# Hi and lo of the latent up-projections staged in the attention's probability tiles as well, until the first latent head begins

## The chip, the core and the metric

The kernel runs on one core of one Trainium2 chip. The metric is the device time of one execution in microseconds. A profile is one execution recorded by the hardware profiler. Engines are named as in the profile: PE is TensorE's matmuls, PEld its weight loads, DVE VectorE, ACT ScalarE, POOL GpSimd, and SP the engine whose queue issues nearly all transfers.

## What is computed

A two-layer encoder over two sequences of 512 tokens (width 1024). The first layer mixes with grouped-query and differential attention, the second with latent attention; each layer then has cross attention to a memory and a gated feed-forward part. The change lies in the latent attention of the second layer:

```python
def mla(h, w_in, g_q, g_kv, w_uq, w_ukv, ang):
    a = h @ w_in
    cq, ckv, kr = jnp.split(a, [C_Q_RANK, C_Q_RANK + C_KV_RANK], axis=-1)
    q = (rms_norm(cq, g_q) @ w_uq).reshape(B, S, C_HEADS, C_NOPE + C_ROPE)
    qn, qr = q[..., :C_NOPE], rope(q[..., C_NOPE:], ang)
    kv = (rms_norm(ckv, g_kv) @ w_ukv).reshape(B, S, C_HEADS, C_NOPE + C_VDIM)
    kn, v = kv[..., :C_NOPE], kv[..., C_NOPE:]
    ...
    # per head: softmax((qn kn + qr kr) * scale) @ v, 16 heads
```

## The kernel before

Activations lie transposed, features on the partitions and 512 tokens along the free dimension; `b` is the sequence. Every float32 operand x is kept as two parts, hi (x rounded) and lo (x minus hi), and a product is three matmuls: hi hi, hi lo, lo hi (`gemm`, `gemm_k`, L126 to L128 and L738 to L740). A product ends in one of three PSUM tiles (`pg`).

The latent stage runs so. `mla_in` projects down and normalises. `mla_up` then makes, for each quarter `u` of the heads, the queries (`qn`, four products of 9 matmuls of 512 columns), for every second quarter the rotated query parts (`rope_q`, four products of 9), the keys (`keys`, four products of 6) and the values (`values`, four products of 12 matmuls of 256 columns, each evicted in two halves). The rotated parts pass through f tiles: two multiplications on DVE and a sum on POOL each. Every result is split into hi and lo in one staging tile (tag `hl`): ACT writes hi, DVE writes lo (L817 and L818, L96 and L97, L848 and L849), and SP then stores the tile to DRAM, from where the heads load it again in another layout. The `hl` tag has two buffers of 128 x 1024 floats. A quarter takes 20 of these tiles: 4, 4, 4 and 8.

The first quarter runs alone (`until(up, lambda: 0 in done)`); the other quarters are woven into the heads of sequence 0. A head (`attend64`) takes four query blocks: scores into one of two `pss` tiles (L909 to L911), the minimum on DVE (L433), the exponential on ACT (L436), scaling on POOL (L441), transposes on PE (L447), hi and lo of the transposed probabilities into two tiles of tag `pt` (L449, L450), and the product with the values (L479, L481). Tag `pt` has four buffers of the same 128 x 1024 floats. Before the heads, `mla_in` uses them for three projections and, at its two ends, for the spread of the norms (`e`).

The order of instructions on each engine is fixed when the kernel is built: the Tile framework schedules the program against a timeline that it models, so a change in buffers moves instructions of several engines. Each engine and the SP queue then work strictly in that order. A wait for a tile that still has to be stored is the wait for its last transfer to land.

Of the kernel before, what the change touches and what calls it, by code (L numbers as in the profile page):

```python
# [10 lines left out]
F32R = mybir.dt.float32r  # L11
# [8 lines left out]
T = 512  # L20
# [14 lines left out]
def trunk_kernel(ctx, tc, xt, memt, gains, lams, w_in0, w_out0, w_in1, w_uq, w_ukv, w_out1,  # L35
# [21 lines left out]
    def nm(s):  # L57
        uid[0] += 1
        return f"{s}{uid[0]}"
# [5 lines left out]
    def f_tile():  # L65
        return f_p.tile([128, T], F32, tag="f", name=nm("f"))
# [9 lines left out]
    def raw(ap):  # L76
        return ap.bitcast(F32)
# [17 lines left out]
    def split(hi, lo, f, eng=None):  # L95
        nc.scalar.copy(hi, f)  # L96
        (eng or nc.vector).tensor_tensor(out=lo, in0=f, in1=raw(hi), op=SUB)  # L97
# [4 lines left out]
    def load_w(src, n=1024, first=False, key=None):  # L102
        r = wr_p.tile([128, 1024], F32, tag="wr", name=nm("wr"))
        h = wh_p.tile([128, 1024], F32R, tag="wh", name=nm("wh"))
        l = wl_p.tile([128, 1024], F32R, tag="wl", name=nm("wl"))
        if key in los:
            dma(r, src)
            dma(raw(l), los.pop(key))
            nc.scalar.copy(h, r)
            return lambda i, n=1: (h[:, i * 128:(i + n) * 128], l[:, i * 128:(i + n) * 128])  # L110
        step = 256 if first else n
        for c in range(0, n, step):
            cs = slice(c, c + step)
            dma(r[:, cs], src[:, cs])
            nc.scalar.copy(h[:, cs], r[:, cs])  # L115
            (nc.vector if first else nc.gpsimd).tensor_tensor(out=l[:, cs], in0=r[:, cs],  # L116
                                                              in1=raw(h[:, cs]), op=SUB)
        if key is not None:
            los[key] = d = dram([128, 1024])
            dma(d, raw(l))  # L120
        return lambda i, n=1: (h[:, i * 128:(i + n) * 128], l[:, i * 128:(i + n) * 128])

    def gemm(ps, ws, xs):
        n = len(ws)
        for i, ((wh, wl), (xh, xl)) in enumerate(zip(ws, xs)):
            nc.tensor.matmul(ps, lhsT=wh, rhs=xh, start=(i == 0), stop=False)  # L126
            nc.tensor.matmul(ps, lhsT=wh, rhs=xl, start=False, stop=False)  # L127
            nc.tensor.matmul(ps, lhsT=wl, rhs=xh, start=False, stop=(i == n - 1))  # L128
# [221 lines left out]
    def cross_kv(l, at):  # L350
# [6 lines left out]
        for m in range(KC):  # L357
            w = load_w(w_ckv[l, m])
            p = pg()
            gemm(p, [w(k) for k in range(KC)], mem)  # L360
            f = f_tile()
            nc.vector.tensor_tensor(out=f, in0=p, in1=Rm[0], op=MUL)
            hl, hi, lo = hl2(at)
            split(hi, lo, f)
            kd[l][m] = d = dram([128, 2, T])
            dma(d, raw(hl))
            yield 5.2
# [141 lines left out]
    skB = [[dram([128, 2, T]) for _ in range(4)] for _ in range(2)]  # L509
    svB = [[dram([2, 128, T]) for _ in range(4)] for _ in range(2)]  # L510

    def hl2(at):
        x = at.tile([128, 2 * T], F32R, tag="hl", name=nm("hl"), bufs=2)
        return x, x[:, :T], x[:, T:]

    def tt(eng, out, a, b, op):
        eng.tensor_tensor(out=out, in0=a, in1=b, op=op)  # L517
# [219 lines left out]
    def gemm_k(o, wh, wl, xh, xl, first, last, **k):  # L737
        nc.tensor.matmul(o, lhsT=wh, rhs=xh, start=first, stop=False, **k)  # L738
        nc.tensor.matmul(o, lhsT=wh, rhs=xl, start=False, stop=False, **k)  # L739
        nc.tensor.matmul(o, lhsT=wl, rhs=xh, start=False, stop=last, **k)  # L740
# [68 lines left out]
        return c_hl  # L809

    def mla_up(at, c_hl, done):
        def qn(w, i, j):
            for b in range(2):
                p = pg()
                gemm(p, [w(i * 3 + k) for k in range(3)], c_hl[b][0:3])
                hl, hi, lo = hl2(at)
                nc.scalar.activation(hi, p, AF.Copy, scale=MLA_SCALE)  # L817
                nc.vector.scalar_tensor_tensor(out=lo, in0=p, scalar=MLA_SCALE, in1=raw(hi),  # L818
                                               op0=MUL, op1=SUB)
                dma(sqn[b][j], raw(hl))  # L820
                yield 1.95

        def keys(w, i, j):
            for b in range(2):
                p = pg()
                gemm(p, [w(i * 2 + k) for k in range(2)], c_hl[b][3:5])
                hl, hi, lo = hl2(at)
                split(hi, lo, p)
                dma(skn[b][j], raw(hl))
                yield 1.4  # L830

        def values(w, u):

            wv = [w(4 + 2 * k, 2) for k in range(2)]
            for b in range(2):
                for tp in range(2):
                    p = pg()
                    for j in range(2):
                        t = tp * 2 + j
                        for k in range(2):  # L840
                            xh, xl = (x[:, t * 128:(t + 1) * 128] for x in c_hl[b][3 + k])
                            gemm_k(p[:, j * 256:(j + 1) * 256], xh, xl, *wv[k], k == 0, k == 1)
                    for j in range(2):
                        t = tp * 2 + j
                        x = at.tile([128, 2 * T], F32R, tag="hl", name=nm("hl"), bufs=2)[:, :T]
                        xv = x.rearrange("p (h s e) -> p h s e", h=4, s=2)
                        pv = p[:, j * 256:(j + 1) * 256].rearrange("p (h e) -> p h e", h=4)
                        nc.scalar.copy(xv[:, :, 0], pv)  # L848
                        nc.vector.tensor_tensor(out=xv[:, :, 1], in0=pv, in1=raw(xv[:, :, 0]),  # L849
                                                op=SUB)  # L850
                        dma(svn[b][u][:, :, t * 128:(t + 1) * 128].rearrange("h p c -> p h c"),
                            raw(x).rearrange("p (h c) -> p h c", h=4))
                    yield 1.4

        def rope_q(g):
            w = load_w(w_uq[4 + g][:, :768], 768)
            cs = at.tile([128, 2 * T], F32, tag="kk", name=nm("ropeC"), bufs=2)
            cos, sin = cs[:, :T], cs[:, T:]
            dma(cos, rope_c[0])
            dma(sin, rope_c[1])  # L860
            for b in range(2):
                eo = []
                for i in range(2):
                    p = pg()
                    gemm(p, [w(i * 3 + k) for k in range(3)], c_hl[b][0:3])
                    eo.append(p)
                for i in range(2):
                    x, y = f_tile(), f_tile()
                    tt(nc.vector, x, eo[i], cos, MUL)
                    tt(nc.vector, y, eo[1 - i], sin, MUL)  # L870
                    tt(nc.gpsimd, x, x, y, SUB if i == 0 else ADD)
                    hl, hi, lo = hl2(at)
                    split(hi, lo, x)
                    dma(sqr[b][g][:, i], raw(hl))
                yield 3.9

        for u in range(4):
            j = 2 * u
            w = load_w(w_uq[j // 2][:, :768], 768)
            for i in range(2):  # L880
                yield from qn(w, i, j + i)
            if u % 2 == 0:
                yield from rope_q(u // 2)
            w = load_w(w_ukv[j // 2])
            for i in range(2):
                yield from keys(w, i, j + i)
            yield from values(w, u)
            done.append(u)
# [425 lines left out]
    with ExitStack() as es:  # L1314
        at = es.enter_context(tc.tile_pool(name="at0", bufs=4))
# [12 lines left out]
        done = []  # L1328
# [14 lines left out]
    with ExitStack() as es:  # L1343
        at = es.enter_context(tc.tile_pool(name="at1", bufs=4))
        nq[0], nv[0] = 4, 2
        c_hl = mla_in(at)
        done = []
        up = mla_up(at, c_hl, done)
        o = [[], []]
        until(up, lambda: 0 in done)  # L1350
        kr = mla_kr(at, 0)
        for u in range(4):
            until(up, lambda: u in done)
            weave(mla_attn(at, 0, kr, range(2 * u, 2 * u + 2), o[0], "B"), up, 1.0)
        first = proj_residual(0, w_out1, ("mix", 1), o[0], next_x(0, G_CROSS + 8, "C"))
        weave(mla_attn(at, 1, mla_kr(at, 1), range(8), o[1], "A"), first, 0.30)
        ops = XOps(1)
        oc = after_mixing(at, 1, w_out1, o, first, ops)
# [123 lines left out]
```

## Time and profile before

| | |
|---|---|
| time, median of 3 runs | 3066.44 us (3065.6 to 3070.57) |
| profiled execution, its own time | 3070.69 us |
| profiled execution, span of its instructions | 3068.9 us |
| PE busy | 2936.0 us, 96% of the span |
| DVE, ACT, POOL busy | 66%, 45%, 54% |
| granted TensorE clock, mean | 0.983 |
| DMA | 500 MB, 163 GB/s over the span |

The profiled execution's own time is what compares with the runs; its span leaves out about 2 us around the first and last instruction. Positions below are microseconds from the span's start. The latent up-projections begin at about 1694 us, the first latent scores at 1739 us, and the last heads end at about 2140 us.

### The profile page before, as it was taken

To read this page: it belongs to the slowest core of one execution; us is meant where nothing else is said; L and a number is where in the kernel's file an instruction comes from. 1 tells how busy PE (TensorE), PEld (TensorE's weight loads), DVE (VectorE), ACT (ScalarE), POOL (GpSimd) and SP (SyncE) were. 2 spreads that over 40 slices of the span, in tenths; PEclk is the share of its full clock that TensorE was granted. 3 is DMA by queue.
4 is the path that set the end of the run, shared out by engine and by line. 5 is a ranking of instruction groups with operands and counts; after the bars stand their busy time and mean duration, and the time that the engine had idled before them with its cause. 6 is when DMAs were issued, how large, how long until landed. Compare 5 with 4: busy or idle time off the path is not lost. (4 is left out here: it accounts for less than half of the span.)

```text
span 3068.9 us, 42037 instructions
## 1 busy us (share of the span) xinstructions
PE 2936.0 (96%) x14301; PEld 2425.2 (79%) x14301; DVE 2029.7 (66%) x3417; ACT 1391.6 (45%) x2610; POOL 1654.2 (54%) x1222
## 2 busy tenths in 40 slices
PE   8999999999999999998999799999999999999996
PEld 6878899877887888876777688888887788887775
DVE  7566766665467665678774576666458666669776
ACT  3245456545344333343343366656444333334342
POOL 5453445443256666667674343553355666666665
PEclk9999999999999999999999999999999999999998
DMA  3554554656573222245341677764756222226442
GB/s 137 166 174 158 189 206 141 228 194 207 185 244 110 103 103 103 103 153 174 132 161 65 209 270 262 241 209 158 247 189 216 96 103 103 99 98 208 138 152 81
DMA packets 217958, 500.01 MB, mean 163 GB/s; under 512 B 22800, under 2 KB 48784, under 8 KB 217744
## 3 DMA queue, kind: packets, MB, share of 16 engines
q1 hardware_dynamic: 217600, 497.28, 47.2%
q8 instruction: 114, 1.87, 0.2%
q14 instruction: 100, 0.82, 0.1%
q10 hardware_dynamic: 144, 0.04, 0.0%
HBM read 341.00 MB, written 156.24 MB: 162 GB/s over the span
## 5 line engine op out<-in xcount | busy, mean ns | idle before, releaser
L126 PE MATMUL pg<-u,wh 128*128 128x512 f32 x1360 | 541.6, 400 | 19.8 <-DVE hl L97 5.2
L128 PE MATMUL pg<-u,wl 128*128 128x512 f32 x1360 | 538.7, 397 | 7.1 <-DMA wl<-dram 4.7
L127 PE MATMUL pg<-u,wh 128*128 128x512 f32 x1360 | 539.1, 397 | 5.2 <-DVE u L242 4.8
L441 POOL TENSOR_SCALAR p<-p,rs 128x512 f32<-128x512 f32 (+1 forms) x288 | 190.6, 665 | 461.0 <-DVE rs L437 380.3
L116 POOL TENSOR_TENSOR wl<-wr,wh 128x1024 fp32r<-128x1024 f32 (+1 forms) x112 | 275.8, 2464 | 271.0 <-ACT wh L115 264.0
L96 ACT CAST s<-ws 128x512 fp32r<-128x512 f32 (+2 forms) x304 | 170.5, 563 | 331.6 <-POOL ws L517 112.2
L126 PEld LDWEIGHTS pg<-u,wh 128*128 128x128 f32 x1360 | 258.6, 190 | 78.7 <-DVE hl L818 6.6
L128 PEld LDWEIGHTS pg<-u,wl 128*128 128x128 f32 x1360 | 257.8, 190 | 61.4 <-DMA wl<-dram 6.2
L127 PEld LDWEIGHTS pg<-u,wh 128*128 128x128 f32 x1360 | 257.9, 190 | 60.0 <-DVE u L242 9.5
L97 DVE TENSOR_TENSOR s<-ws,s 128x512 fp32r<-128x512 f32 x176 | 175.8, 1000 | 90.9 <-ACT s L96 90.9
L436 ACT ACTIVATE p<-p,mx 128x512 f32<-128x512 f32 (+1 forms) x256 | 171.5, 670 | 111.1 <-DVE mx L433 103.6
L449 ACT CAST ptt<-pt 128x512 fp32r<-128x512 f32 (+1 forms) x288 | 151.4, 536 | 130.4 <-PE pt L447 128.7
L450 DVE TENSOR_TENSOR ptt<-pt,ptt 128x512 fp32r<-128x512 f32 (+1 forms) x288 | 177.6, 624 | 39.7 <-ACT ptt L449 38.0
L738 PE MATMUL pss<-u,s 128*128 128x512 f32 x484 | 191.7, 397 | 6.9 <-ACT s L96 3.4
L237 POOL TENSOR_TENSOR ssq<-ssq,f 128x512 f32<-128x512 f32 x100 | 149.3, 1497 | 90.6 <-ACT f L235 88.0
L740 PE MATMUL pss<-u,s 128*128 128x512 f32 x484 | 192.3, 397 | 1.1 <-DVE s L97 1.1
L517 POOL TENSOR_TENSOR f<-f,c 128x512 f32<-128x512 f32 x88 | 148.6, 1690 | 81.4 <-DVE f L517 78.3
L739 PE MATMUL pss<-u,s 128*128 128x512 f32 x484 | 191.7, 396 | 0.0
L115 ACT CAST wh<-wr 128x1024 fp32r<-128x1024 f32 (+2 forms) x120 | 118.5, 993 | 160.9 <-PE pg L127 105.3
L97 POOL TENSOR_TENSOR s<-ws,s 128x384 fp32r<-128x384 f32 (+1 forms) x128 | 145.2, 1141 | 76.7 <-ACT s L96 75.4
L738 PE MATMUL pg<-u,s 128*128 128x512 f32 x440 | 175.3, 398 | 6.2 <-ACT s L96 2.8
L739 PE MATMUL pg<-u,s 128*128 128x512 f32 x440 | 174.5, 397 | 2.0 <-DVE u L517 2.0
(300 smaller groups left out, 7840.5 us busy)
## 6 DMA issues: line engine op xcount, KB each, us to landing
dram<-hl SPq DMA_DIRECT2D x88, 512.0 KB, 3.0
wr<-in_w_gu_dram SPq DMA_DIRECT2D x88, 512.0 KB, 3.3
u<-dram SPq DMA_DIRECT2D x154, 256.0 KB, 3.6
dram<-f SPq DMA_DIRECT2D x152, 256.0 KB, 2.7
kk<-dram SPq DMA_DIRECT2D x52, 512.0 KB, 4.9
q<-dram SPq DMA_DIRECT2D x96, 256.0 KB, 4.3
dram<-wl SPq DMA_DIRECT2D x48, 512.0 KB, 2.9
wl<-dram SPq DMA_DIRECT2D x48, 512.0 KB, 4.3
```

Source lines behind the costliest of these rows:

```text
L96: nc.scalar.copy(hi, f)
L97: (eng or nc.vector).tensor_tensor(out=lo, in0=f, in1=raw(hi), op=SUB)
L116: (nc.vector if first else nc.gpsimd).tensor_tensor(out=l[:, cs], in0=r[:, cs], in1=raw(h[:, cs]), op=SUB)
L126: nc.tensor.matmul(ps, lhsT=wh, rhs=xh, start=(i == 0), stop=False)
L127: nc.tensor.matmul(ps, lhsT=wh, rhs=xl, start=False, stop=False)
L128: nc.tensor.matmul(ps, lhsT=wl, rhs=xh, start=False, stop=(i == n - 1))
L436: nc.scalar.activation(p, p, AF.Exp, bias=mn, scale=-1.0, accum_out=su)
L441: nc.gpsimd.tensor_scalar(out=p, in0=p, scalar1=rs, scalar2=1.0, op0=MUL, op1=MUL)
L450: nc.vector.tensor_tensor(out=pl, in0=tv, in1=raw(ph), op=SUB)
L738: nc.tensor.matmul(o, lhsT=wh, rhs=xh, start=first, stop=False, **k)
L739: nc.tensor.matmul(o, lhsT=wh, rhs=xl, start=False, stop=False, **k)
L740: nc.tensor.matmul(o, lhsT=wl, rhs=xh, start=False, stop=last, **k)
```

## The change

`mla_up` takes its staging tiles through a counter. While no quarter is done (`done` is empty, which is the first quarter's 20 tiles), two of three tiles are taken from the four buffers of tag `pt` and the third from the two of `hl`; later quarters use `hl` alone, as before. The arithmetic stays as it is.

```diff
--- before.py
+++ after.py
@@ -509,8 +509,8 @@
     skB = [[dram([128, 2, T]) for _ in range(4)] for _ in range(2)]
     svB = [[dram([2, 128, T]) for _ in range(4)] for _ in range(2)]
 
-    def hl2(at):
-        x = at.tile([128, 2 * T], F32R, tag="hl", name=nm("hl"), bufs=2)
+    def hl2(at, tag="hl"):
+        x = at.tile([128, 2 * T], F32R, tag=tag, name=nm("hl"), bufs=4 if tag == "pt" else 2)
         return x, x[:, :T], x[:, T:]
 
     def tt(eng, out, a, b, op):
@@ -809,11 +809,18 @@
         return c_hl
 
     def mla_up(at, c_hl, done):
+
+        turn = [0]
+
+        def up_hl():
+            turn[0] += 1
+            return hl2(at, "pt" if not done and turn[0] % 3 else "hl")
+
         def qn(w, i, j):
             for b in range(2):
                 p = pg()
                 gemm(p, [w(i * 3 + k) for k in range(3)], c_hl[b][0:3])
-                hl, hi, lo = hl2(at)
+                hl, hi, lo = up_hl()
                 nc.scalar.activation(hi, p, AF.Copy, scale=MLA_SCALE)
                 nc.vector.scalar_tensor_tensor(out=lo, in0=p, scalar=MLA_SCALE, in1=raw(hi),
                                                op0=MUL, op1=SUB)
@@ -824,7 +831,7 @@
             for b in range(2):
                 p = pg()
                 gemm(p, [w(i * 2 + k) for k in range(2)], c_hl[b][3:5])
-                hl, hi, lo = hl2(at)
+                hl, hi, lo = up_hl()
                 split(hi, lo, p)
                 dma(skn[b][j], raw(hl))
                 yield 1.4
@@ -842,7 +849,7 @@
                             gemm_k(p[:, j * 256:(j + 1) * 256], xh, xl, *wv[k], k == 0, k == 1)
                     for j in range(2):
                         t = tp * 2 + j
-                        x = at.tile([128, 2 * T], F32R, tag="hl", name=nm("hl"), bufs=2)[:, :T]
+                        x = up_hl()[0][:, :T]
                         xv = x.rearrange("p (h s e) -> p h s e", h=4, s=2)
                         pv = p[:, j * 256:(j + 1) * 256].rearrange("p (h e) -> p h e", h=4)
                         nc.scalar.copy(xv[:, :, 0], pv)
@@ -869,7 +876,7 @@
                     tt(nc.vector, x, eo[i], cos, MUL)
                     tt(nc.vector, y, eo[1 - i], sin, MUL)
                     tt(nc.gpsimd, x, x, y, SUB if i == 0 else ADD)
-                    hl, hi, lo = hl2(at)
+                    hl, hi, lo = up_hl()
                     split(hi, lo, x)
                     dma(sqr[b][g][:, i], raw(hl))
                 yield 3.9
```

The built order of the instructions moves with it. Names are tile and number; `hl_16373`, `hl_16387`, `hl_16401`, `hl_16415` are the staging tiles of the first four query products (`pg_16363` to `pg_16405`), and `hl_16249`, `hl_16289` those of the key rotation at the end of `mla_in`. Lines of the changed kernel are 7 higher from here on.

ACT at the start of the up-projections, before:

```order
L96 CAST hl_16289<-f_16285 32x512
L817 ACTIVATE hl_16373<-pg_16363 128x512
L196 COPY r_16328<-pa_16323 128x512
L196 COPY r_16335<-pt_16330 128x512
L96 CAST u_16338<-c_16086 128x512
L817 ACTIVATE hl_16387<-pg_16377 128x512
L96 CAST u_16343<-c_16150 128x512
L115 CAST wh_16505<-wr_16504 128x1024
L96 CAST u_16348<-c_16140 128x512
L817 ACTIVATE hl_16401<-pg_16391 128x512
L96 CAST u_16353<-c_16205 128x512
```

and in the changed kernel:

```order
L824 ACTIVATE hl_16373<-pg_16363 128x512
L824 ACTIVATE hl_16387<-pg_16377 128x512
L96 CAST hl_16289<-f_16285 32x512
L824 ACTIVATE hl_16401<-pg_16391 128x512
L196 COPY r_16328<-pa_16323 128x512
L196 COPY r_16335<-pt_16330 128x512
L96 CAST u_16338<-c_16086 128x512
L115 CAST wh_16505<-wr_16504 128x1024
L96 CAST u_16343<-c_16150 128x512
L824 ACTIVATE hl_16415<-pg_16405 128x512
```

The first three query evictions now stand together, ahead of the copies of the norms (L196) and the splits of the key and value latents (`u`); before, the second to fourth stood between those.

PE where the first latent scores (`pss_16672`, head 0, block 0) begin; `pg_16596` is the third product of the first quarter's values, `pg_16691` the second query product of the second quarter. Before:

```order
L739 MATMUL pg_16596<-wl_16506,u_16353 128x256
L740 MATMUL pg_16596<-wh_16505,u_16354 128x256
L909 MATMUL pss_16672<-kk_16662,q_16661 128x512
L910 MATMUL pss_16672<-kk_16662,q_16661 128x512
L911 MATMUL pss_16672<-kr_16658,q_16663 128x512
```

and in the changed kernel:

```order
L127 MATMUL pg_16691<-u_16077,wh_16639 128x512
L128 MATMUL pg_16691<-u_16076,wl_16640 128x512
L916 MATMUL pss_16672<-kk_16662,q_16661 128x512
L917 MATMUL pss_16672<-kk_16662,q_16661 128x512
L918 MATMUL pss_16672<-kr_16658,q_16663 128x512
```

Three products moved ahead of the first scores: the fourth of the values (`pg_16617`) and two of the second quarter's queries (`pg_16644`, `pg_16691`).

ACT where the first exponentials stand (`p_16679` is head 0, block 0; `hl_16567` to `hl_16634` are the eight halves of the first quarter's values). Before:

```order
L96 CAST hl_16550<-pg_16543 128x512
L848 CAST hl_16567<-pg_16554 128x4x64
L436 ACT_TABLE_LOAD
L436 ACTIVATE p_16679,su_16677<-p_16679,mx_16676 128x512
L436 ACTIVATE p_16712,su_16710<-p_16712,mx_16709 128x512
L848 CAST hl_16571<-pg_16554 128x4x64
```

and in the changed kernel:

```order
L855 CAST hl_16592<-pg_16575 128x4x64
L115 CAST wh_16842<-wr_16841 128x1024
L855 CAST hl_16609<-pg_16596 128x4x64
L855 CAST hl_16613<-pg_16596 128x4x64
L855 CAST hl_16630<-pg_16617 128x4x64
L436 ACT_TABLE_LOAD
L436 ACTIVATE p_16679,su_16677<-p_16679,mx_16676 128x512
L824 ACTIVATE hl_16654<-pg_16644 128x512
```

The exponentials stood behind the first of the eight value halves and now stand behind the seventh (`hl_16630`), with the split of a weight tile (`wh_16842`) between.

## Rows read from the trace of the kernel before

**Rows 1.** The page of the profiled execution: its span, and its part 1 (busy time of each engine, its share of the span, its instructions).

```profile
span 3068.9 us, 42037 instructions
...
PE 2936.0 (96%) x14301; PEld 2425.2 (79%) x14301; DVE 2029.7 (66%) x3417; ACT 1391.6 (45%) x2610; POOL 1654.2 (54%) x1222
```

**Rows 2.** Busy time by stretch, a stretch per row: its length, then for PE, PEld, DVE, ACT and POOL the busy us and, in brackets, the instructions, then the granted TensorE clock (1.00 is full), the mean busy share of the 16 DMA engines, and GB/s.

```profile
1700.00:1740.00 40.00, 27.58 (x120) 21.02 (x119) 20.73 (x30) 12.40 (x21) 12.63 (x8) 0.87 0.63 218
1740.00:1780.00 40.00, 36.17 (x200) 29.32 (x199) 25.50 (x68) 26.27 (x58) 13.80 (x16) 1.00 0.78 264
...
1850.00:1950.00 100.00, 94.55 (x564) 81.05 (x562) 66.19 (x176) 65.43 (x149) 38.95 (x46) 0.98 0.71 236
1950.00:2050.00 100.00, 100.00 (x551) 85.75 (x550) 66.94 (x156) 64.48 (x125) 61.32 (x50) 1.00 0.72 248
```

**Rows 3.** Waits of PE between 1693 and 1746 us: the matmul that waited, by tile and line, what released it, us in total, times, the longest.

```profile
PE pg L126 <- DVE hl L97: 5.2, 1, 5.2
PE pg L126 <- DVE hl L818: 4.4, 3, 2.3
PE pg L738 <- DVE hl L97: 2.3, 1, 2.3
PE pss L909 <- DVE mx L433: 1.4, 1, 1.4
PE pt L447 <- POOL p L441: 1.1, 1, 1.1
```

**Rows 4.** PE in order of time: start, us, engine, line, operation, tiles, forms, and in brackets the idle time ahead of it with its releaser. The matmuls of 128x512 follow each other in one product, so the distance of two starts is what one costs.

```profile
1702.87 0.50 PE L126 MATMUL pg<-u,wh 128*128 128x512 f32 x1 [1.40 <-DVE hl L818]
...
1707.49 0.50 PE L126 MATMUL pg<-u,wh 128*128 128x512 f32 x1 [2.28 <-DVE hl L818]
...
1708.30 0.39 PE L126 MATMUL pg<-u,wh 128*128 128x512 f32 x1
1708.53 0.40 PE L127 MATMUL pg<-u,wh 128*128 128x512 f32 x1
...
1713.02 0.50 PE L126 MATMUL pg<-u,wh 128*128 128x512 f32 x1 [0.71 <-DVE hl L818]
...
1727.56 0.80 PE L126 MATMUL pg<-u,wh 128*128 128x512 f32 x1 [5.16 <-DVE hl L97]
...
1729.01 0.63 PE L126 MATMUL pg<-u,wh 128*128 128x512 f32 x1
1729.43 0.63 PE L127 MATMUL pg<-u,wh 128*128 128x512 f32 x1
...
1732.76 0.58 PE L738 MATMUL pg<-wh,u 128*128 128x256 f32 x1 [2.27 <-DVE hl L97]
...
1738.26 0.28 PE L739 MATMUL pg<-wl,u 128*128 128x256 f32 x1
1738.38 0.28 PE L740 MATMUL pg<-wh,u 128*128 128x256 f32 x1
...
1738.86 0.39 PE L909 MATMUL pss<-kk,q 128*128 128x512 f32 x1
...
1745.67 0.66 PE L447 MATMUL pt<-ident,p 128*128 128x128 f32 x4 [1.08 <-POOL p L441]
```

**Rows 5.** ACT in order of time, same columns: two evictions into the staging tile, and the first exponential of the latent attention.

```profile
1731.39 0.58 ACT L96 CAST hl<-pg 128x512 fp32r<-128x512 f32 x1 [4.62 <-DMA dram<-hl]
...
1742.13 0.37 ACT L848 CAST hl<-pg 128x256 fp32r<-128x256 f32 x1 [6.11 <-DMA dram<-hl]
...
1743.81 0.72 ACT L436 ACTIVATE p<-p,mx 128x512 f32<-128x512 f32 x1
```

**Rows 6.** Busy time by stretches of 4 us, columns as in rows 2.

```profile
1722.00:1726.00 4.00, 0.40 (x2) 0.00 (x0) 1.02 (x2) 0.62 (x1) 1.45 (x1) 1.00 0.74 239
1726.00:1730.00 4.00, 2.44 (x6) 1.83 (x6) 0.69 (x1) 0.58 (x1) 0.00 (x0) 0.53 1.02 322
...
1738.00:1742.00 4.00, 3.90 (x21) 2.78 (x19) 1.39 (x4) 0.00 (x0) 0.00 (x0) 1.00 0.84 335
```

**Rows 7.** DMA issues between 1700 and 1746 us: destination and source, queue, count, KB each, median us from issue to landing.

```profile
dram<-hl SPq DMA_DIRECT2D x12, 512.0 KB, 3.5
kk<-dram SPq DMA_DIRECT2D x3, 512.0 KB, 4.6
q<-dram SPq DMA_DIRECT2D x5, 256.0 KB, 5.3
```

**Rows 8.** DVE and then POOL in order of time, columns as in rows 4: evictions, rotations and a weight split of the up-projections.

```profile
1712.28 0.69 DVE L818 SCALAR_TENSOR_TENSOR hl<-pg,hl 128x512 fp32r<-128x512 f32 x1 [2.36 <-ACT hl L817]
1712.88 3.23 DVE L517 TENSOR_TENSOR f<-pg,ropeC 128x512 f32<-128x512 f32 x5
1716.28 1.12 DVE L97 TENSOR_TENSOR hl<-f,hl 128x512 fp32r<-128x512 f32 x1 [0.17 <-ACT hl L96]
...
1714.31 2.54 POOL L517 TENSOR_TENSOR f<-f,f 128x512 f32<-128x512 f32 x2 [1.18 <-DVE f L517]
...
1719.49 2.29 POOL L116 TENSOR_TENSOR wl<-wr,wh 128x768 fp32r<-128x768 f32 x1
```

**Rows 9.** Waits of PE between 1746 and 2290 us, columns as in rows 3: the two largest.

```profile
PE pss L909 <- DMA kk<-dram: 3.1, 2, 2.2
PE pa L479 <- ACT ptt L449: 2.7, 4, 2.0
```

## The prediction, made before the changed kernel ran

> **What bounds the kernel now.** I read the page first: PE is busy 2936.0 of 3068.9 us [rows 1], so the kernel is bound by PE, and an edit is worth what it takes from PE's idle time or slow clock. The busy time by stretch shows where that lies [rows 2]: in the 40 us from 1700 PE is busy only 27.58 us and its clock is granted at 0.87, the worst stretch near the change; from 1950 to 2050 PE is busy without a break, so what is won ahead of 1950 has nothing to be lost in there. Third, the waits of PE around 1700 [rows 3]: 5.2, 4.4 and 2.3 us, 11.9 together, until DVE had written an `hl` tile, since only then a `pg` tile is free for the next product. DVE writes lo after ACT's hi, so fourth ACT: it too sat idle, 4.62 us before the eviction at 1731.39 and 6.11 us before the one at 1742.13, until the store `dram<-hl` had landed [rows 5]. The chain is: a store lands, ACT and DVE evict, a `pg` comes free, PE goes on. Two staging buffers and a store of 3.5 us from issue to landing [rows 7] let through two results per round; PE makes one in 1.4 to 2.1 us. The change hits this chain.
>
> **What is lost there.** Between the end of the norm's transposes (1702.87 less 1.40, so 1701.47) and the first scores at 1738.86 [rows 4], 37.4 us, PE does five products of 9 matmuls (the last query and four rotations), four of 6 (keys) and three of 12 half-width ones (values). At 0.23 us per matmul (1708.30 to 1708.53) and 0.12 (1738.26 to 1738.38) [rows 4] that is 45 x 0.23 + 24 x 0.23 + 36 x 0.12 = 20.2 us. So 17.2 us are lost: 11.9 idle, some 3 at a slower clock after the gap of 5.16 us (the starts at 1729.01 and 1729.43 are 0.42 apart; the clock is 0.53 from 1726 to 1730 [rows 4, 6], the lower level, 1.2 GHz, taking part), and the rest in the first matmul and the tail of every product that stood alone.
>
> **The change, step by step.** It adds no instruction; it gives the first quarter's 20 tiles six buffers in place of two, and the built order moves.
>
> Queries. Their evictions no longer wait for stores, and the first three stand together on ACT. One takes about 0.6 us on ACT (0.58 [rows 5]) and 0.69 on DVE [rows 8], against 2.1 us (9 x 0.23) that PE takes for a product. The gaps of 1.40, 2.28 and 0.71 us [rows 4] go, and PE ends the last query product at about 1703.7 and the third rotation at about 1710.
>
> Rotations. Here DVE is next in line: eight multiplications at 0.65 (five take 3.23), four lo parts of 1.1, and POOL's sums at 1.27 (two take 2.54) behind a weight split of about 2.3 and two latent splits [rows 8]. DVE's order puts the lo of the first rotated part ahead of the last multiplications, so the second key product finds its `pg` free at about 1715.8, when PE could have begun at 1714.0. With two smaller waits behind it I count 3.6 us of idle time that stays, 1714 to 1722. The value products follow, and at 1727.3 the fourth of them is done, which before came only after the first heads had started.
>
> Transfers. Six buffers let stores pile up. By SP's order there lie, from about 1716.5 to the store of the first value half, a weight tile (0.39 MB), seven tiles of 0.52 MB, the first heads' loads of 0.52 x 2 and 0.26 x 2, and that half itself, 0.26: 5.9 MB. The most that moved in 4 us here is 335 GB/s, the mean of a busy stretch 264 [rows 6, 2]. I take the upper, since in this piece transfers are always waiting: 17.6 us, so the store lands at 1734.1. That matters, because six tiles later the seventh value half is in its buffer, and the first exponential stands behind that half on ACT. From the start of an eviction to the first exponential it is 1.68 us (1742.13 to 1743.81 [rows 5]); with a little for the release I put the exponential at 1736.1. Before it was at 1743.81: 7.7 us earlier. PE has by then also done the three products that moved ahead of the scores, 12 x 0.12 + 18 x 0.23 = 5.6 us. Together 13.3.
>
> Start of the heads. Before, PE idled 1.4 and 1.1 us here [rows 3]. Now it waits about 2.3 us ahead of the fifth score, whose `pss` is freed behind the exponential, and about 1.3 us for the `pg` of the third query product, freed by the eighth value half, which ACT does behind three exponentials: 1.1 more than before. Then the probability tiles. The heads take them when the staged values have been stored, and the last store stands on SP behind a query load that waits for head 0's scores (the four `q` tiles are all taken). I expect DVE to wait some 2 us for it; behind it on DVE stand the next minima and evictions, and PE waits for both. So 13.3 - 1.1 - 2 = 10.2, **about 10 us**.
>
> The sum is made on the profiled execution (its own time 3070.69 us, 4.25 above the median of the runs, so 3060.7 for it); on the runs' median of 3066.44 it gives **3056.5 us**. Below 0.2% (6.1 us) a measurement of this kernel can hardly be told from no change.
>
> **A rule on the transfers.** The rows show 335 GB/s as the best of 4 us and 322 at a busy share of 1.02 [rows 6], so I price the pile at 335. The Trainium skill, in "DMA: Bandwidth & Descriptors", section Specifications, puts what one core gets from its memory at about 358 GB/s. By that the 5.9 MB take 16.5 us and the sum is 11.3 us instead of 10.2; and it speaks against more, for keys come at 0.52 MB per 1.4 us, 375 GB/s, which it would not let through however many buffers there are.
>
> **Rivals.**
> The transfers bind harder. If the pile moves at the 264 GB/s of 1740 to 1780 [rows 2], 5.9 MB take 22.3 us, the exponential moves 4.7 us later, and 5.5 us remain. For it: loads of the first heads compete, at 4.6 and 5.3 us to landing [rows 7]. Against: 4 us windows of 322 and 335 [rows 6]. Time: 3061.
>
> The transfers do not bind. Then the walk ends with PE's own 3.6 us of idle, the first scores begin at about 1731 with all evictions on time, and the gain is the 17.2 lost less 3.6, some 14 to 15 us; a loss avoided on `kk` loads [rows 9] could add to it. Time: 3052.
>
> Given back in the heads. From 1746 on PE waits for loads of keys (3.1 us in two waits) and for ACT's probability tiles (2.7) [rows 9]; the stretch 1850 to 1950 has 5.45 us of idle time [rows 2]. If such a chain, and not the amount of work, sets when the heads get through, starting earlier only lengthens their waits until 1950, and a new order adds its own. Against it: PE is 94.55 of 100 busy there, so at most some 5% is slack. Time: 3062 to 3070.
>
> Slower. The heads need the `pt` tiles as soon as they begin, and these now hold values that wait to be stored. DVE stops at the first lo of such a tile, and with it all minima, evictions and PE; SP's order makes the last store wait for the heads' own scores. I priced it at 2 us; it takes the whole gain at 12 us and makes the kernel measurably slower from 18 us. The 6.11 us that ACT once waited for a store [rows 5] is the longest seen, so this takes three such waits in a row. Time: above 3072.6.
>
> That the change does nothing can be left out: at 1701.5 the last `e` tile has been read, so the four `pt` buffers are free when the second query product comes.
>
> **How the numbers follow.** Forecast, 6.2 to 14 us faster: 0.55. Transfers bind harder, 2 to 6.1 us faster: 0.20, of which a few hundredths lie past the bound. Transfers do not bind, 14 to 20 faster: 0.10. Given back, from 2 faster to 6 slower: 0.10. Slower: 0.05. So faster 0.67, same 0.27, slower 0.06. The range from 3049 to 3065 (17.4 to 1.4 us faster) holds the forecast, the harder transfers and most of the third case, a little over 0.8.
>
> **What would show it.** Right: the waits of `pg` for the tiles of L818 and L97 fall from 11.9 to below 5 us up to the first scores; the clock stays at full level from 1722 to 1738; the first scores come at 1731 to 1734 behind three more products, the first exponential at about 1736; DMA moves over 300 GB/s from 1717 to 1735. Wrong: ACT waits for `dram<-hl` well past 1736 ahead of the first exponential; DVE waits several us ahead of L450 for a store; or the idle time of PE between 1746 and 1950 grows by more than 5 us.

## The result, and the profile after

The changed kernel takes 3045.81 us (median of five runs, 3039.9 to 3055.9), the kernel before 3066.44 us (median of five). The ratio is 0.9933, with a 95% interval from 0.9916 to 0.9949: faster by 20.6 us, and by 15.6 to 25.8 us with the interval. The prediction was 3056.5 us with a range from 3049 to 3065: it had the direction, and half of the size.

The page of the changed kernel, its span and part 1, to be read beside [rows 1]:

```profile
span 3044.1 us, 42063 instructions
...
PE 2926.5 (96%) x14301; PEld 2419.1 (79%) x14301; DVE 2028.1 (67%) x3417; ACT 1392.1 (46%) x2610; POOL 1655.1 (54%) x1222
```

The span is 24.8 us shorter, PE is busy 9.5 us less with the same 14301 matmuls, and so idle 15.3 us less. Busy time by stretch of the changed kernel, columns as in [rows 2]:

```profile
1700.00:1740.00 40.00, 33.49 (x161) 26.76 (x160) 23.79 (x46) 18.59 (x37) 18.87 (x13) 0.96 0.89 296
1740.00:1780.00 40.00, 39.98 (x258) 35.46 (x257) 29.52 (x78) 28.93 (x65) 15.26 (x18) 1.00 0.82 284
...
1850.00:1950.00 100.00, 95.18 (x569) 81.15 (x568) 69.77 (x178) 70.26 (x151) 45.91 (x48) 1.00 0.75 248
1950.00:2050.00 100.00, 100.00 (x553) 85.99 (x552) 59.54 (x147) 58.18 (x115) 57.52 (x48) 1.00 0.66 224
```

From 1700 to 1740 PE is busy 33.49 us in place of 27.58, and the transfers move 296 GB/s in place of 218. From 1740 to 1780, where the first heads run, PE has no gap left (39.98 of 40 us; before 36.17). The latent stage begins 3.8 us earlier in this execution (1689.9 in place of 1693.7, shown below), so where a few us matter, times are counted from that start.

The waits of PE from 1693 to 1746 us in the changed kernel, columns as in [rows 3]:

```profile
PE pg L126 <- DVE f L517: 2.8, 1, 2.8
PE pg L738 <- DVE hl L856: 2.2, 1, 2.2
PE pg L738 <- DVE hl L97: 0.9, 1, 0.9
PE pg L126 <- DVE hl L856: 0.4, 1, 0.4
```

The 11.9 us until `hl` tiles of queries, rotations and keys were written have become 0.9 (L97; queries would be L825); 2.6 stand until value halves (L856, before L849) and 2.8 in the rotations (L517) are new.

PE in order of time, columns as in [rows 4]:

```profile
1712.43 0.47 PE L126 MATMUL pg<-u,wh 128*128 128x512 f32 x1 [2.78 <-DVE f L517]
1717.75 0.39 PE L738 MATMUL pg<-wh,u 128*128 128x256 f32 x1 [0.87 <-DVE hl L97]
1724.58 0.48 PE L738 MATMUL pg<-wh,u 128*128 128x256 f32 x1 [2.25 <-DVE hl L856]
...
1732.39 0.39 PE L916 MATMUL pss<-kk,q 128*128 128x512 f32 x1
```

ACT in order of time, columns as in [rows 5]: evictions of value halves, each behind a store, and the first exponential.

```profile
1721.75 0.65 ACT L855 CAST hl<-pg 128x256 fp32r<-128x256 f32 x2 [3.76 <-DMA dram<-hl]
1723.60 0.37 ACT L855 CAST hl<-pg 128x256 fp32r<-128x256 f32 x1 [1.20 <-DMA dram<-hl]
1724.82 0.37 ACT L855 CAST hl<-pg 128x256 fp32r<-128x256 f32 x1 [0.84 <-DMA dram<-hl]
...
1732.46 0.37 ACT L855 CAST hl<-pg 128x256 fp32r<-128x256 f32 x1 [2.83 <-DMA dram<-hl]
...
1734.15 0.73 ACT L436 ACTIVATE p<-p,mx 128x512 f32<-128x512 f32 x1
```

Busy time by short stretches, columns as in [rows 6]:

```profile
1722.00:1726.00 4.00, 1.75 (x10) 1.58 (x10) 1.60 (x4) 1.14 (x4) 0.00 (x0) 0.83 1.01 386
1726.00:1730.00 4.00, 3.84 (x16) 3.01 (x15) 0.76 (x2) 1.69 (x3) 1.43 (x1) 0.74 0.90 271
...
1717.00:1735.00 18.00, 14.52 (x76) 12.33 (x77) 6.06 (x16) 6.52 (x14) 2.38 (x1) 0.91 1.02 348
```

DMA issues from 1700 to 1746 us, columns as in [rows 7]:

```profile
dram<-hl SPq DMA_DIRECT2D x12, 512.0 KB, 5.3
...
kk<-dram SPq DMA_DIRECT2D x3, 512.0 KB, 7.0
```

So the chain was moved, not removed: ACT's value halves still wait for stores to land, and these now land 5.3 us after issue in place of 3.5, behind a pile of other transfers.

**Stages and losses.** The executions of one kernel differ by some 5 us outside the latent stage, so the stage is compared by itself. It runs from the start of the last sum of the norms (L183) to the start of the last product with the values (L481). Line L183, its matmuls with the first and last start, then the last L481, of the kernel before:

```profile
L183 PE MATMUL pa<-cols,ssq x48: 164/250/250, 36.5 to 1693.7; 128*128 128x1 f32 x48
...
2142.45 0.28 PE L481 MATMUL pa<-ptt,vt 128*128 128x256 f32 x1
```

and of the changed kernel:

```profile
L183 PE MATMUL pa<-cols,ssq x48: 164/250/250, 37.2 to 1689.9; 128*128 128x1 f32 x48
...
2119.86 0.28 PE L481 MATMUL pa<-ptt,vt 128*128 128x256 f32 x1
```

The stage takes 448.7 us before and 430.0 after: 18.7 of the 24.8 us between the two spans lie in it, the rest is such a difference. The first scores come 45.2 us into it before (1738.86) and 42.5 after (1732.39).

The loss of a head is worked out from PE's order of time: from its first score to that of the next head, less the matmuls in between at the distance they have when nothing is in the way (0.228 us for 512 columns, 0.1195 for 256, 0.0885 for a transpose of 128). It holds waits, stretched matmuls and slow clock alike. Heads are counted over both sequences, 0 to 31; the first sixteen are those with woven products. Eight matmuls of one column in the second sequence are not taken off. Where an expectation names a loss, it lies within 0.4 us of the table. All fourteen profiles, in us; "ahead" counts the products of the values' end and the second quarter that PE does before the first scores:

| kernel | to first scores | ahead | heads | stage | loss of heads 0 to 2 | 3 to 15 | 16 to 30 | time, ratio to before |
|---|---|---|---|---|---|---|---|---|
| before | 45.2 | 0 | 403.5 | 448.7 | 6.6 | 18.2 | 11.7 | 3066.44 |
| r_before | 46.2 | 0 | 404.1 | 450.3 | 5.4 | 19.8 | 11.8 | 3064.81, one run |
| after | 42.5 | 3 | 387.5 | 430.0 | 1.7 | 14.3 | 10.0 | 0.9933 (0.9916 to 0.9949) |
| r_after | 41.8 | 3 | 388.7 | 430.5 | 2.4 | 14.5 | 10.2 | 3054.23, one run |
| e1_ahead | 58.7 | 3 | 389.3 | 448.0 | 2.8 | 13.5 | 11.4 | 1.001 (0.9998 to 1.0021) |
| e2_back | 39.6 | 1 | 396.6 | 436.2 | 3.6 | 16.4 | 10.9 | 0.994 (0.9916 to 0.9964) |
| e3_first8 | 39.5 | 0 | 407.5 | 447.0 | 6.0 | 23.1 | 11.4 | 0.9989 (0.9977 to 1.0002) |
| e4_last12 | 48.7 | 3 | 388.4 | 437.1 | 0.9 | 14.6 | 11.3 | 0.9968 (0.9957 to 0.9978) |
| e5_ratio13 | 45.8 | 0 | 405.9 | 451.7 | 6.0 | 21.5 | 11.4 | 0.9996 (0.9984 to 1.0009) |
| e7_allpt | 41.9 | 3 | 386.9 | 428.8 | 2.4 | 11.6 | 11.4 | 0.9933 (0.9911 to 0.9955) |
| e8_more | 48.7 | 5 | 384.7 | 433.4 | 1.5 | 14.5 | 11.4 | 0.9953 (0.9935 to 0.997) |
| e9_quarter | 41.6 | 3 | 391.5 | 433.1 | 5.3 | 13.3 | 11.4 | 0.9942 (0.9921 to 0.9963) |
| e6_after13 | 42.0 | 3 | 393.8 | 435.8 | 2.2 | 18.7 | 11.3 | 3056.23, one run |
| e10_ratio08 | 47.0 | 0 | 399.2 | 446.2 | 5.5 | 15.4 | 11.3 | 3069.55, one run |

With the means of the two executions of each kernel the stage gains 449.5 - 430.2 = 19.3 us. The way to the first scores gives 45.7 - 42.15 = 3.55, and the work done by then, three products of 5.6 us, comes on top: 9.1. The heads 0 to 2 lose 4.0 us less, the heads 3 to 15 4.6 less, the second sequence 1.6 less. These sum to 19.3; the last head, which has no next one, is not counted.

The buffers and not the order make most of it: the kernel before takes 446.2 to 451.7 us for the stage in three orders (before, r_before, e5_ratio13, e10_ratio08), and with all twenty tiles of the first quarter in six buffers it takes 428.8 to 436.2 (after, r_after, e2_back, e6_after13, e7_allpt). The two ranges lie 10 us apart.

### The profile page after: what moved, and what is told of

Read it like the earlier page. It is cut to its first block, busy times and chain, and to the rows that moved or that the text cites. A ratio compares the mean times of both kernels' runs of the same rounds, so it can differ in the third digit from the quotient of the medians.

```text
span 3044.1 us, 42063 instructions
## 1 busy us (share of the span) xinstructions
PE 2926.5 (96%) x14301; PEld 2419.1 (79%) x14301; DVE 2028.1 (67%) x3417; ACT 1392.1 (46%) x2610; POOL 1655.1 (54%) x1222
## 5 line engine op out<-in xcount | busy, mean ns | idle before, releaser
L441 POOL TENSOR_SCALAR p<-p,rs 128x512 f32<-128x512 f32 (+1 forms) x288 | 191.7, 669 | 415.1 <-DVE rs L437 333.5
L97 DVE TENSOR_TENSOR s<-ws,s 128x512 fp32r<-128x512 f32 x176 | 173.6, 988 | 90.5 <-ACT s L96 90.5
L517 POOL TENSOR_TENSOR f<-f,c 128x512 f32<-128x512 f32 x88 | 149.2, 1697 | 81.8 <-DVE f L517 78.6
L97 POOL TENSOR_TENSOR s<-ws,s 128x384 fp32r<-128x384 f32 (+1 forms) x128 | 144.7, 1137 | 73.8 <-ACT s L96 68.3
L738 PE MATMUL pg<-u,s 128*128 128x512 f32 x440 | 174.8, 397 | 6.2 <-ACT s L96 2.9
L433 DVE CUSTOM_DVE_ANT_0 p<-pss,cols 128x512 f32<-128x512 f32 (+1 forms) x192 | 113.6, 597 | 98.5 <-PE pt L447 74.6
```

The source lines that it names most:

```text
L441: nc.gpsimd.tensor_scalar(out=p, in0=p, scalar1=rs, scalar2=1.0, op0=MUL, op1=MUL)
```

## Experiments

The expectations stand as they were written, each with the theories of that moment.

**The two kernels again**, for what repeats. No edit.

> The kernel before, profiled once more, for the spread. The latent stage is taken from the last matmul that sums the norms (L183) to the last product with the values (L481): 448.7 us in the first profile of before (45.2 to the first scores, 403.5 from there), 430.0 in that of the change (42.5 and 387.5). Both theories: 448.7 within 2 us, with waits for the loads of keys in the heads again.

> The changed kernel, profiled once more. Both theories: the stage takes 430.0 us within 2 us, 42.5 of them up to the first scores.

Measured: stages of 450.3 and 430.5 us, 1.6 and 0.5 us from the first profiles, and losses within 1.7. Before and behind the stage the two changed executions differ by 3.0 and 4.7 us. What follows: the stage and its parts may be read to about 2 us, while one time of a whole execution says less than that.

**Is it the work ahead, or the buffers?** The first kernel keeps two buffers and holds the first scores back behind the first two query products of the second quarter:

```diff
         until(up, lambda: 0 in done)
+        next(up)
+        hold[0] = last[0]
...
+                    with tc.issue_after(hold[0].ins) if first else ExitStack():
                         nc.tensor.matmul(s, lhsT=q[:, ts], rhs=khh, start=True, stop=False)
```

> Two staging buffers as before, but the first scores are held on PE behind the two query products of the second quarter, as the change has them. Theory A (the heads lose less because the products of the later quarters run ahead of them): the first scores come some 10 to 13 us later than before, at 55 to 58 us of the stage, and the heads take at most 391 us, so the stage is 446 to 449 us, no longer than before. Theory B (the heads gain by the order that came with six buffers, by chance, and not by the lead): the heads take 398 us, before's less the work moved ahead, and the stage 453 to 456 us, slower than before by 5 to 8 us.

The other is the changed kernel with the same two products held behind the first scores, and with one more `yield` at the end of each quarter, so that they are written behind the scores that they wait for:

```diff
+                with tc.issue_after(score0[0].ins) if (b, j) == (0, 2) else ExitStack():
                     gemm(p, [w(i * 3 + k) for k in range(3)], c_hl[b][0:3])
```

> Six staging buffers as in the change, but the two query products of the second quarter are held behind the first scores. Theory A: the first scores come at about 38 us of the stage, the heads lose what they lost before and take about 402 us, the stage 440 us, 10 us slower than the change. Theory B: the heads take what they take in the change and the two products, about 392 us, the stage 430 us, as fast as the change.

With two buffers and three products ahead the time is that of before (3070.98 us, ratio 1.001): the way to the first scores is 13.0 us longer, of which only 5.6 is work, and the heads give 14.5 back. The heads lose less although two buffers hold the value halves, which here are all evicted ahead of the first exponential. The waits of PE from 1739 to 1945 us in this kernel (L852 is the lo of a value half) show where most of the rest goes, the 5.1 ahead of the first scores:

```profile
PE pg L739 <- DVE hl L852: 5.1, 1, 5.1
PE pg L126 <- DVE hl L852: 2.4, 3, 1.7
```

Behind it stands ACT, here from 1693 to 1775 us:

```profile
ACT hl L851 <- DMA dram<-hl: 15.1, 8, 5.8
```

All eight value halves wait for stores, 15.1 us together, and the place of PE's wait has moved from the heads to ahead of them. With six buffers and one product ahead the first scores come 2.6 us earlier than in the changed kernel, the heads take 8.5 us more, of which 4.1 is the work of the two products, and the stage is 6 us longer. So the buffers with just one product ahead carry about two thirds of the stage's gain (449.5 to 436.2), though the time of the runs can't tell this kernel from the change (0.994 beside 0.9933), and putting work ahead without buffers gains nothing. Theory A had the stage of e1_ahead (448.0), and neither theory that of e2_back, which lies between their 440 and 430.

**Which tiles?** Probability tiles for the first eight tiles alone (queries and rotated parts), and for the last twelve alone (keys and values):

```diff
-            return hl2(at, "pt" if not done and turn[0] % 3 else "hl")
+            return hl2(at, "pt" if not done and turn[0] <= 8 and turn[0] % 3 else "hl")
```

```diff
-            return hl2(at, "pt" if not done and turn[0] % 3 else "hl")
+            return hl2(at, "pt" if not done and turn[0] > 8 and turn[0] % 3 else "hl")
```

> The change for the first eight tiles alone (queries and rotations of the first quarter); keys and values use the two staging buffers. PE's time over its work is now counted head by head; in heads 0 to 2 before lost 5.4 to 6.6 us in two profiles, the change 1.3 to 2.1. Theory C (heads 0 to 2 lose because value halves of the first quarter still wait for two buffers on ACT, ahead of the exponentials; the later heads lose by how the later quarters happen to stand among them): heads 0 to 2 lose 5 to 7 us as before, the way to the first scores shortens by about 4 us, the stage is 443 to 446 us. Theory D (the whole gain in the heads comes with the time won ahead of them): heads 0 to 15 lose some 4 us less than before in proportion to the 4 us won.

> The change for the last twelve tiles alone (keys and values of the first quarter). Theory C: heads 0 to 2 lose about 2 us as in the change, the first scores come 4 us later than in the change, at 46 us of the stage with three products done ahead, and the stage is 433 to 436 us. Theory D: the gain of the heads is half that of the change, the stage 438 us or more.

With the first eight the first scores come 6.2 us earlier than before, and the time is hardly another (ratio 0.9989): heads 0 to 2 lose 6.0 us, as before, and heads 3 to 15 lose 23.1, where the two executions of before lost 18.2 and 19.8. The waits of PE from 1739 to 1945 us in it (L441 is POOL's scaling; L97 and L856 are lo parts behind stores):

```profile
PE pt L447 <- POOL p L441: 3.0, 1, 3.0
PE pg L738 <- DVE hl L97: 2.3, 3, 1.7
PE pg L126 <- DVE hl L856: 2.1, 3, 1.5
PE pss L916 <- DMA kk<-dram: 1.5, 2, 0.8
```

With the last twelve the way to the first scores is 48.7 us, and 43.1 without the three products that are in it; heads 0 to 2 lose only 0.9, and the stage gains 12.4 us. Alone the two parts give 2.5 and 12.4, together 19.3. Most of what e3_first8 won to the first scores was lost again in heads 3 to 15, as the rival "given back in the heads" had it; whether the two buffers or its own order took it is not shown, since order alone moves these heads by some 4 us (below). What the pair does show is heads 0 to 2: 6.0 us with the value halves in two buffers among the heads, 0.9 with them in six buffers and ahead. Theory D, that the heads gain with the time won ahead of them, falls with e3_first8, and with e1_ahead and e2_back.

**The order by itself.** The kernel before with another ratio in the weave is built in another order and leaves its buffers and the products ahead of the first scores as they were:

```diff
-            weave(mla_attn(at, 0, kr, range(2 * u, 2 * u + 2), o[0], "B"), up, 1.0)
+            weave(mla_attn(at, 0, kr, range(2 * u, 2 * u + 2), o[0], "B"), up, 1.3)
```

> The kernel before, two staging buffers throughout, with the later quarters woven into the heads of sequence 0 at 1.3 instead of 1.0 of their due work, which moves them to other places. Theory C: heads 0 to 2 lose 5 to 7 us as before; heads 3 to 15, which lost 18.0 to 19.7 us in two profiles of before and 14.0 to 14.1 in those of the change, lose anything from 13 to 22 us by their order alone, more than 2 us off before's. Theory E (two buffers set what the later heads lose, whatever the order): 18 to 20 us again.

The time stays (0.9996). Heads 0 to 2 lose 6.0 us, as before, and heads 3 to 15 lose 21.5, more than the 18 to 20 of theory E.

**More of the same.** Probability tiles in all quarters:

```diff
-            return hl2(at, "pt" if not done and turn[0] % 3 else "hl")
+            return hl2(at, "pt" if turn[0] % 3 else "hl")
```

> The change without its end at the first head: all four quarters stage two of three tiles in the probability tiles, which the heads use at the same time. Theory E: with six buffers for the later quarters too, heads 3 to 15 lose 10 us or less in place of 14. Theory C: heads 3 to 15 lose as much as in the change or more, since heads and projections now wait for each other's tiles; the stage is 428 to 436 us.

The ratio is that of the change, 0.9933, and the stage 1.4 us shorter, which is no difference: from the second quarter on six buffers are worth nothing that can be measured. Heads 3 to 15 lose 11.6 us, which neither theory had.

All four query products of the second quarter ahead of the first scores, in six buffers (the hold of e1_ahead on the changed kernel, with `for _ in range(3): next(up)` and `"pt" if turn[0] <= 24 and turn[0] % 3 else "hl"`), and the whole second quarter written ahead of the first head:

```diff
-        until(up, lambda: 0 in done)
+        until(up, lambda: 1 in done)
...
-            return hl2(at, "pt" if not done and turn[0] % 3 else "hl")
+            return hl2(at, "pt" if len(done) < 2 and turn[0] % 3 else "hl")
```

> The change, with all four query products of the second quarter ahead of the first scores instead of two, and these staged in the six buffers too. So far heads 3 to 15 lost 11.4 to 14.5 us in the four kernels that have three products ahead of the first scores, whether two or six buffers stage them, 16.0 with one ahead and 18.0 to 22.8 in the four profiles with none. Theory A (how far the later quarters run ahead of the heads sets it): with five ahead heads 3 to 15 lose 9 to 12 us; the first scores come at 46 to 48 us of the stage; the stage is 426 to 430 us. Theory C (order by chance): heads 3 to 15 lose 14 us or more as likely as less, the stage 429 to 434 us.

> The change, with the whole second quarter traced ahead of the first head and staged in the six buffers; in the built order the same three products stand ahead of the first scores, but 28 us of the later quarters' work, in place of 7, ahead of head 2. Theory A: heads 3 to 15 lose less than in the change, 8 to 12 us. Against it stand the probability tiles, which the first heads now share with the second quarter: heads 0 to 2 lose 2 to 8 us. The stage is 425 to 435 us. Theory C: heads 3 to 15 lose 12 to 18 us.

Both miss what the theory of the lead expected: five products ahead leave the later heads' loss at 14.5, and in the second kernel the built order puts just three ahead of the first scores again, with 13.3. The stages are 3 us longer than after the change. More lead than the change gives is not worth more.

**Lead, or the luck of the order?** By then every kernel with three products ahead or more had lost 11.6 to 14.6 us in heads 3 to 15, and every one with none 18.2 to 23.1. Two more orders were made to break this: the changed kernel with the ratio at 1.3, the kernel before with 0.8 (the line edited is that of e5_ratio13).

> The changed kernel with the weave's ratio at 1.3 instead of its own, which lays some 1,500 instructions in another order and leaves six buffers and three products ahead of the first scores. Theory A (the heads after the third lose little where products run ahead of the first scores): heads 0 to 2 lose 1 to 3 us, heads 3 to 15 lose 11 to 15 us, and no wait on a late key load. Theory C (the later heads' loss is the luck of the order): heads 3 to 15 fall anywhere between 11 and 23 us.

> The kernel before with the weave's ratio at 0.8, which lays some 2,000 instructions in another order and leaves two buffers and no product ahead of the first scores. Theory A: heads 0 to 2 lose 5 to 7 us, heads 3 to 15 lose 18 us or more, with waits on late key loads as before. Theory C: heads 3 to 15 fall anywhere between 11 and 23 us.

Both broke it: 18.7 us with three ahead, 15.4 with none, each in one profile. The waits of PE in the first, from 1731 to 1945 us:

```profile
PE pss L916 <- DVE mx L433: 2.4, 6, 0.6
PE pt L447 <- POOL p L441: 2.2, 1, 2.2
PE pss L916 <- DMA kk<-dram: 1.3, 2, 0.7
```

and in the second:

```profile
PE pg L738 <- DVE hl L97: 4.1, 1, 4.1
PE pt L447 <- POOL p L441: 3.1, 3, 1.2
...
PE pss L909 <- DMA kk<-dram: 1.1, 1, 1.1
```

The 4.1 us of the second lie ahead of its first scores, at 1741.36. The late key loads (`kk`) stand in the first though its products run ahead. So theory A as a rule falls: the loss of heads 3 to 15 moves by some 4 us with the order alone, in either direction (14.4 to 18.7 after, 19.0 to 15.4 or 21.5 before), and of the 4.6 us that the change won there at least a part belongs to the order in which it happened to be built. Heads 0 to 2 held to what was expected in both, 2.2 and 5.5. At one ratio of 1.3 for both kernels the change is worth 451.7 - 435.8 = 15.9 us in the stage, at 1.0 it is worth 19.3.

## Why the prediction came out too small

**The chain was right.** Stores that land late keep ACT and DVE from evicting, and so `pg` from PE. Waits of `pg` for L97 and for the queries' lo fell from 11.9 to 0.9 us, and the first scores came behind exactly the three products named. In e3_first8 and e4_last12 the two halves of the chain show apart. That the first scores stand at 1732.39, in the 1731 to 1734 forecast, is luck: the forecast was made on the profile of before, where the stage starts at 1693.7, so it says 37.3 to 40.3 us into the stage, and they came at 42.5 and 41.8 in the two executions.

**What stays in the rotations.** 3.6 us were forecast between 1714 and 1722; 2.78 and 0.87 are what stayed, at 1712.43 and 1717.75 of PE's order of time, which is 1716.2 and 1721.5 if the stage starts as in before. The size was right; the cause of the first was another, a rotation that waits for DVE's multiplications, not a key product.

**The transfers.** They bound as forecast: ACT waited 3.76, 1.20 and 2.83 us for stores, the last directly ahead of the first exponential, and 348 GB/s moved from 1717 to 1735, where 335 had been taken. But 335 was not the most of 4 us in the kernel before: its own trace has 355 and 400, in no row shown (columns as in [rows 2]):

```profile
1727.00:1731.00 4.00, 2.93 (x6) 1.83 (x6) 0.50 (x1) 0.00 (x0) 0.00 (x0) 0.50 0.98 355
1812.00:1816.00 4.00, 4.00 (x23) 3.38 (x22) 2.09 (x4) 1.08 (x2) 2.03 (x1) 1.00 1.03 400
```

The Trainium skill, in "DMA: Bandwidth & Descriptors", Specifications, puts one core's share of its memory at about 358 GB/s. The 348 over 18 us lie close to it, but the 386 of 1722 to 1726 are above it, and so are the 400 before; the measurement decides, so the remark that keys at 375 GB/s would not be let through however many buffers there are did not hold over 4 us. That transfers bind harder (264) or not at all are both out; the second rival's own sum, 17.2 less 3.6, gives 13.6 us and not 14 to 15. The first exponential came 1734.15 - 1689.9 = 44.25 us into the stage, before 1743.81 - 1693.7 = 50.1: 5.9 us earlier, where 7.7 were forecast. With the 5.6 us of products that is 11.5 for 13.3, and what was missed here stands ahead of the first scores: PE still waits 2.25 us for a value half at 1724.58, and the clock was not full from 1722 to 1738 but 0.83 and 0.74 for 8 us, the lower level of 1.2 GHz taking part.

**Start of the heads: the step that failed first.** It took off 1.1 and 2 us for new waits. Neither came: PE has no gap from 1740 to 1780, and DVE's wait ahead of the first probability tiles is small. The row of DVE's waits from 1725 to 1800 us that answers to it:

```profile
DVE ptt L450 <- PE pa L479: 0.6, 1, 0.6
```

It is for PE, not for a store; the rival "slower" hung on this wait. What the step left out is that before, the same heads lost 5.4 to 6.6 us, of which it named 2.5 [rows 3], and that much of this came from the change's own cause: seven of the eight value halves stood among the first exponentials on ACT, in two buffers. ACT's waits for stores ahead of the first quarter's halves, from the first scores on, before (1738 to 1764 us):

```profile
ACT hl L848 <- DMA dram<-hl: 10.8, 4, 6.1
```

and after (1732 to 1764 us):

```profile
ACT hl L855 <- DMA dram<-hl: 2.8, 1, 2.8
```

Before, 6.11 us of the 10.8 stood ahead of the first exponential and 4.7 among the exponentials and casts of the first heads; after, the 2.83 ahead of the first exponential are all. The halves did not stop waiting: with the 3.76, 1.20 and 0.84 us that came earlier, ACT waited 8.6 us for their stores. What changed is the place. Heads 0 to 2 lose 5.4 to 6.6 us wherever seven of the eight halves are evicted behind the first exponential (before, r_before, e3_first8, e5_ratio13, e10_ratio08), and 0.9 to 3.6 where six or more are evicted ahead of it, in two buffers too (e1_ahead, 2.8, which pays ahead of the first scores). Only e9_quarter, 5.3 with seven ahead, does not fit, and it has a whole quarter more written ahead. From the first exponential (11.5 us gained) to the end of head 2 (9.1 + 4.0 = 13.1) the gain grew by 1.6, where it was to shrink by 3.1. That is 4.7 us of the miss, of which the exponential above takes back 1.8.

**Later heads: the step that was missing.** The sum put nothing there. The kernel won 4.6 us in heads 3 to 15 and 1.6 in the second sequence, the larger part of the miss. The prediction saw the rows, 3.1 us of waits for `kk` and 2.7 for ACT [rows 9], but wrote them into rivals only: a loss avoided on `kk` "could add to it", without a price. After the change the waits of PE from 1732 to 1930 us hold no `kk`, and ACT's is small:

```profile
PE pss L916 <- DVE mx L433: 1.8, 4, 0.9
PE pg L738 <- DVE hl L856: 1.8, 1, 1.8
...
PE pa L479 <- ACT ptt L449: 0.2, 1, 0.2
```

With the two terms, 13.1 and 6.2, the gain is 19.3 in place of 10.2. How much of the 4.6 us is the head start and how much the order stays open: kernels without products ahead lost 15.4 to 23.1 us (four orders), those with three or more 11.6 to 18.7 (seven orders), which speaks for a share of the head start, and the two ranges overlap. The 1.6 of the second sequence look like the order of this one build: every other kernel lost 10.9 to 11.8 there, those with six buffers too, and only the changed one 10.0 and 10.2. In hindsight a sounder form of this term was 0 with some 4 us to either side, which would have moved the range's lower end from 3049 to about 3045.

**Given back** did not happen in the changed kernel; in e3_first8, where only the first half of the chain went, the heads took back most of it. From 1950 to 2050 PE is busy without a break in both kernels, as the prediction read it.

## What to carry to other kernels

When staging buffers hold up a producer, follow the same tag past the point where the next phase begins: here the last of its tiles stood among the next phase's work on the same engine, and moving them ahead of it was worth 4 us in the first three heads. Price a gain in the later phase as well as a loss, and where a change lets instructions be laid out anew, give that phase a term of its own size (here some 4 us to either side); running the kernel before in another order is a cheap way to learn that size. Judge such a change by the stage that it touches, which repeated within 1.6 us, and not by spans that differ by several us elsewhere. And compare two profiles from a common event: positions from the span's start had shifted by 3.8 us, enough to make a missed place look met.

## What the runs showed of the hardware

The transfers of one core moved 348 GB/s over 18 us and 386 over 4 us, at a DMA share of 1.02 and 1.01; the kernel before reached 400 over 4 us, from 1812 to 1816, at a share of 1.03. With the pile the time from issue to landing of a 512 KB store went from 3.5 to 5.3 us, and of a key load from 4.6 to 7.0. And the clock fell to 0.83 and then 0.74 around a gap of only 2.25 us that followed one of 0.87, while before it was still 1.00 from 1722 to 1726, with PE busy 0.40 us in it, and 0.53 only in the next 4 us, at the end of the gap of 5.16 [rows 4, 6].
